# New places for out-projection and RWKV steps, two more MLP pairs ahead of their operands, and the second product's first split inside the last pair, in a hybrid layer

## Chip, cores and metric

The kernel runs on one core of a Trainium2 chip. The metric is the device time of one execution in microseconds; of several runs the median is shown. The engines are named as the profile names them: PE (matrix products), PEld (its weight loads), DVE (VectorE), ACT (ScalarE), POOL (GpSimd) and SP, whose queue issues nearly all transfers.

## What is computed

One layer on 1024 positions of width 1024, in float32. The input is normalised and projected to 3200 features in one product; four mixers of width 256 work on slices of them (chunked attention with a relative bias, HGRN2, RWKV-7, RG-LRU); their outputs are joined, projected back, normalised and added to the input; a squared-ReLU MLP with 4096 hidden features follows. Cut to the part around the change:

```python
mix = jnp.concatenate([ya, yb, yc, yd], axis=-1).astype(dt)
x = x + rms_norm(mix @ w_out[l], norm_mix_post[l])
h = rms_norm(x, norm_mlp_pre[l])
ff = jnp.square(jax.nn.relu(h @ mlp_w1[l])) @ mlp_w2[l]
x = x + rms_norm(ff, norm_mlp_post[l])
```

## The kernel before, in words

**Precision.** Every large product is made of three: each operand is split into a high part (a cast on ACT) and a low part (source minus high part, on DVE), and PE sums high x high, high x low and low x high into one PSUM bank (mm1, line 1159, for the MLP's first product; mm2 for its second). "Splitting" means that cast and that subtraction.

**Stages.** The 1024 positions are two halves of 512. For each half the mixers run (order RALH, then RHAL) and write their outputs to DRAM (mixd). part2 (line 1121) begins with the out projection: out_load (1049) fetches and splits the mixers' outputs of a half, out_mm (1060) multiplies, residual (1089) normalises and adds. For half 0, h2t (1281) transposes the result y0 into B1, eight pairs of split tiles. For half 1 the result is y1.

**The first MLP product** goes over 16 pairs of hidden tiles (a pair is two tiles of 128 features) by a scheme of seven products instead of eight over the 2 x 2 blocks of the operands (hidden tiles x inner index against the two halves of positions; Winograd's form). B1 is half 0's operand; Bt[0..4] are its sums and differences with half 1, made from y1 in the block marked T (lines 1336 to 1356): 32 transposes on PE, 36 sums and subtractions on DVE, 28 casts and scalings on ACT, the last of them for Bt[4]. Every product of 128 x 512 over half the inner index is 12 matmuls. A pair goes in steps: up_first (1200) loads the first weights, splits A11 and A12, and makes the product a, copied to s1; up_c11 (1210) adds the second product to a and gives h11; up_rest (1217) is a generator with five yields: split of s1's operand; product c with Bt[1], copied to s5 (line 1228); product b with Bt[2], s6 = s1 + b; product d with Bt[3], s5 += d; c with Bt[0], giving h21; d with Bt[4], then h22, h12 and the sums that the second product needs, each written to DRAM (put, 1179). w2_sums (1182) does sums of the second weights alongside. up_first and up_c11 need B1 alone, so for the first NFILL pairs they run ahead, while y1 is still on its way (fill, 1308); such a pair loads its first weights again later and its h11 back from DRAM.

**The second MLP product** (product, 1418) goes over seven block products of eight steps q. Each step loads two operands, splits both (split2, 1394) and makes 24 matmuls (lines 1414 to 1416).

**Memory.** Tiles come from pools; a tile tag with n buffers is a ring of n. Pool pw1 holds from part2 to the end: raw weights "wr" (4 buffers), split tiles "hl" (6), "s1" (6), "ho". Pool psc (1360) opens only after the raw inputs of T (raw0, raw1) are closed, and takes over their memory: s5, s6 (lines 1227, 1233), ho2, w2s, and more split tiles "hl2" (NHL3 = 2 before). hl (1138) counts the split tiles and sends them to one ring or the other:

```python
nhl[0] += 1
if hl2 and nhl[0] % (NHL + hl2[-1][1]) >= NHL:
    t = hl2[-1][0].tile([P, 2, 512], F32R, tag="hl2", name=nm(name), bufs=hl2[-1][1])
else:
    t = pw1.tile([P, 2, 512], F32R, tag="hl", name=nm(name), bufs=NHL)
```

**Order.** Every instruction has a place, its number in program order. A block entered with high_priority(offset=n) stands n places ahead; at(key) enters such a block with the offset that PRIO gives for the key (lines 56 to 61 and 102), and without an entry the offset is 0. A planner at build time goes through modelled time and gives each engine the ready instruction with the lowest place; what comes out is a fixed order for each engine, and each engine keeps its own. Keys that the change touches: "Om" + half (out_mm), "Rn" + half (rwkv's normalisation and gating, line 678), "U" + pair, and two new ones.

Of the kernel before, what the change touches and what calls it, by code (L numbers as in the profile page):

```python
# [43 lines left out]
GELU_C = math.sqrt(2.0 / math.pi)  # L44
DECAY_C = math.exp(-0.5)
PRIO_UP = 200
NFILL = 4
NWR, NHL, NHO, NS1, NHL2, NHL3, NHO2, NR2, NXR, NJ = 4, 6, 2, 6, 12, 2, 6, 8, 4, 2
KORD = ((0, 1, 2, 3, 4, 5, 6, 7), (4, 5, 6, 7, 2, 3, 0, 1))
PO0 = (("fm", "fm", "pa", "pa"), ("fm", "fm", "pa", "pa"))  # L50
PO1 = (("fm", "fm", "pa", "pa"), ("py", "fm", "pa", "ph"))
# [1 line left out]
NTAIL = 2  # L53
ORDER = ("RALH", "RHAL")

PRIO = {"A0": 30, "Ah01": 200, "Ah10": 100, "Ah11": 400, "Ah20": 60, "Ah30": 365, "At0": 700, "At1": 400, "Hf0": 40,
# [5 lines left out]
LEVELS = (32, 16, 8, 4, 2, 1)  # L62

VEC = {}
# [25 lines left out]
def body(ctx: ExitStack, tc: tile.TileContext, A: dict, out: bass.AP, dbg=None, stop_after=None):  # L90
# [11 lines left out]
    def at(*key):  # L102

        sec.close()
        n = PRIO.get("".join(map(str, key)), 0)
        if n:
            sec.enter_context(tc.high_priority(offset=n))

    def nm(base):
        uid[0] += 1  # L110
        return f"{base}_{uid[0]}"
# [1009 lines left out]
    def part2():  # L1121
# [10 lines left out]
        def raw(name):  # L1132
            return pw1.tile([P, 1024], F32, tag="wr", name=nm(name), bufs=NWR)
# [83 lines left out]
        def up_rest(p, r0, a, s1, w12):  # L1217
            if p < NFILL:
                r0 = w1load(2 * p)
            r1 = w1load(2 * p + 1)  # L1220
            A11, A12, A21, A22 = r0[:, 0:512], r0[:, 512:], r1[:, 0:512], r1[:, 512:]
            V.tensor_tensor(A21, A21, A22, ADD)
            w = parts(A21, "s1", V)
            yield
            c = bankm("pc_")
            mm1(c, w, Bt[1], True, True)
            s5 = psc.tile([P, 512], F32, tag="s5", name=nm("s5"), bufs=2)
            S.copy(s5[:], c[:])
            yield
            V.tensor_tensor(A21, A21, A11, SUB)  # L1230
            b = bankm("pb_")
            mm1(b, parts(A21, "s2", V), Bt[2], True, True)
            s6 = psc.tile([P, 512], F32, tag="s6", name=nm("s6"), bufs=2)
            V.tensor_tensor(s6[:], s1[:], b[:], ADD)
            yield
            V.tensor_tensor(A11, A22, A21, SUB)
            d = bankm("pd_")
            mm1(d, parts(A11, "s3", V), Bt[3], True, True)
            V.tensor_tensor(s5[:], s5[:], d[:], ADD)
            yield  # L1240
            if p >= NFILL:
                h11 = up_c11(p, a, w12)
            else:
                h11 = ho("ho")
                nc.sync.dma_start(h11[:], hx[0][p // 2][:, p % 2, :])
            V.tensor_tensor(A12, A12, A21, SUB)
            mm1(c, parts(A12, "s4", V), Bt[0], False, True)
            h21 = ho2("h21")
            V.tensor_tensor(h21[:], s6[:], c[:], ADD)
            relu2(h21[:], h21[:])  # L1250
            yield
            mm1(d, parts(A22, "w22", V), Bt[4], False, True)
            w2_sums(p)
            h22 = ho2("h22")
            V.tensor_tensor(h22[:], s6[:], s5[:], ADD)
            relu2(h22[:], h22[:])
            put(p, 3, h22)
            h12 = ho2("h12")
            V.tensor_tensor(h12[:], s6[:], d[:], ADD)
            relu2(h12[:], h12[:])  # L1260
            put(p, 1, h12)

            t1, t2, t4 = ho2("t1"), ho2("t2"), ho2("t4")
            V.tensor_tensor(t1[:], h21[:], h22[:], ADD)
            V.tensor_tensor(h21[:], h11[:], h21[:], SUB)
            V.tensor_tensor(t2[:], t1[:], h11[:], SUB)  # L1266
            V.tensor_tensor(t4[:], h12[:], t2[:], SUB)
            for i, t in ((4, t1), (6, h21), (5, t2), (2, t4)):
                put(p, i, t)
# [35 lines left out]

        fst = []

        def fill(n):

            for p in range(0, n, 2):  # L1310
                q = range(p, min(p + 2, n))
                for p in q:
                    fst.append(up_first(p))
                for p in q:
                    up_c11(p, fst[p][1], fst[p][3])

        with tc.high_priority(offset=PRIO_UP):
            fill(NFILL)
        part1.close()
        pb1_ = ctx2.enter_context(ExitStack())  # L1320
        pb1 = pb1_.enter_context(tc.tile_pool(name="pb1", bufs=1, reuse_waits="tile"))
# [6 lines left out]
        def bsplit(i, k, src, eng):  # L1328
            split(eng, Bt[i][k][0][:], Bt[i][k][1][:], src)

        gens = [up_rest(p, *fst[p]) for p in range(2)]
        with tc.high_priority(offset=PRIO_UP):
            for x in gens:
                next(x)
        kh = range(4)
        at("T")
        b12, b22 = [z[:] for z in raw1[0:4]], [z[:] for z in raw1[4:8]]
# [16 lines left out]
        for k in kh:  # L1354
            V.tensor_tensor(b11[k], b21[k], b11[k], SUB)
            bsplit(4, k, b11[k], V)
        at()
        raw1_.close()
        raw0_.close()
# [3 lines left out]
        while gens:  # L1363
            for x in list(gens):
                if next(x, 1):
                    gens.remove(x)
        for p in range(2, NHID // 2):
            at("U", p)
            for _ in up_rest(p, *(fst[p] if p < NFILL else up_first(p))):
                pass  # L1370
        at()
        ctx2.close()

# [15 lines left out]
        def load(src, name):  # L1389
            r = raw2(name)  # L1390
            nc.sync.dma_start(r[:], src)
            return r

        def split2(r, name):

            h, l = hl(name), hl(name)
            h_, l_ = (z[:].rearrange("p a b -> p (a b)") for z in (h, l))
            S.copy(h_, r[:])  # L1398
            V.tensor_tensor(l_, r[:], h_.bitcast(F32), SUB)  # L1399
            return h, l  # L1400

        W2 = lambda c: (lambda q: load(A["w2"][c, q], "wb"))
        TX = lambda i: (lambda q: load(tx[i][q][:].rearrange("p a b -> p (a b)"), "wt"))
# [14 lines left out]
        def product(i, right, banks, start, tail=0):  # L1418

            ops = {}  # L1420
            for q in range(NQ):
                x = split2(load(hx[i][q][:].rearrange("p a b -> p (a b)"), "ha"), "a2")
                ops[q] = x, split2(right(q), "b2")
                if q >= NQ - tail:
                    continue
                for t in range(4):
                    for n in range(2):
                        mm2(banks, *ops[q], t, n, start and q == 0 and n == 0, q == NQ - 1 and n == 1)
            for t in range(4):
                for q in range(NQ - tail, NQ):  # L1430
                    for n in range(2):
                        mm2(banks, *ops[q], t, n, False, q == NQ - 1 and n == 1)
                if tail:
                    yield t
# [195 lines left out]
```

## Time and profile before

| | us |
|---|---|
| median of 3 runs | 1336.4 |
| lowest and highest | 1330.17 and 1336.4 |
| the profiled execution, its own time | 1338.78 |
| its span, first to last instruction | 1337.0 |
| PE busy in the span | 1264.3 |
| mean granted clock of PE | 0.969 of full |

The profile is of one execution, and times within it are microseconds from the span's start. The mixers of both halves fill the first 620 us and more, the out projection runs from about 577 to 683, the first MLP product from 683 to 1014, the second from there to 1330. In the rows below, "<-" in brackets behind an instruction names what ended the idle time of its engine before it; matmuls overlap, so the duration of one is longer than the distance between two starts.

### The profile page before, as it was taken

The page shows a single profiled execution, that of the slowest core. Times are in us where ns is not written, and L with a number is a line of the kernel's source. Part 1 is how long each engine was busy: PE and PEld are TensorE (multiplying, and loading weights), DVE is VectorE, ACT ScalarE, POOL GpSimd, SP SyncE. Part 2 cuts the span into 40 slices and gives each one's busy share as a digit, 9 for nine tenths or more (in the row PEclk, how much of TensorE's full clock was granted, in tenths as well). Part 3 has the DMA queues.
Part 4 walks back from the last instruction along what each step waited for, and adds up shares of the span by engine and source line. Part 5 has one row for each costly group of instructions (what it writes and reads, how often), then busy time and mean ns, then how long its engine had stood idle before and what let it go on. Part 6 is the DMA issues. An engine that isn't in the chain of part 4 may idle for free. (4 is left out here: it accounts for less than half of the span.)

```text
span 1337.0 us, 21742 instructions
## 1 busy us (share of the span) xinstructions
PE 1264.3 (95%) x8424; PEld 995.1 (74%) x8424; DVE 852.7 (64%) x1538; ACT 662.0 (50%) x1171; POOL 83.7 (6%) x115
## 2 busy tenths in 40 slices
PE   6899999799999999998997999999998999999997
PEld 4677779566687777666786878888887888888886
DVE  4763647677553486765768878876775444444884
ACT  6633646466444344755766545454454433433441
POOL 1000010314102150000000000000000000000000
PEclk9898999889898999999998999999998999999999
DMA  7432112222122012334832888776656875666751
GB/s 261 137 95 74 34 63 93 81 67 92 41 86 70 18 56 74 91 120 139 312 136 76 287 296 267 265 267 233 214 197 241 322 257 194 194 192 197 262 227 63
DMA packets 101160, 213.66 MB, mean 160 GB/s; under 512 B 25281, under 2 KB 28993, under 8 KB 101057
## 3 DMA queue, kind: packets, MB, share of 16 engines
q1 hardware_dynamic: 101056, 212.27, 47.1%
q8 instruction: 66, 1.08, 0.3%
q14 instruction: 38, 0.30, 0.1%
HBM read 156.92 MB, written 55.31 MB: 159 GB/s over the span
## 5 line engine op out<-in xcount | busy, mean ns | idle before, releaser
L1414 PE MATMUL q<-b,a 128*128 128x512 f32 x448 | 175.8, 394 | 2.4 <-ACT b L1398 2.4
L1415 PE MATMUL q<-b,a 128*128 128x512 f32 x448 | 176.7, 394 | 1.3 <-DVE b L1399 1.3
L1416 PE MATMUL q<-b,a 128*128 128x512 f32 x448 | 176.4, 394 | 0.0
L324 PE MATMUL fm<-hh,wh 128*128 128x512 f32 x304 | 130.0, 430 | 13.2 <-ACT wh L182 8.0
L325 PE MATMUL fm<-hh,wl 128*128 128x512 f32 x304 | 128.0, 425 | 0.9 <-DVE wl L184 0.9
L326 PE MATMUL fm<-hl,wh 128*128 128x512 f32 x304 | 125.7, 419 | 0.5 <-DVE hl L253 0.5
L184 DVE TENSOR_TENSOR wl<-wr,wh 128x1024 fp32r<-128x1024 f32 x66 | 81.3, 1234 | 46.9 <-ACT wh L182 46.4
L182 ACT CAST wh<-wr 128x1024 fp32r<-128x1024 f32 x66 | 69.0, 1045 | 68.4 <-PE fm L326 37.6
L1414 PEld LDWEIGHTS q<-b,a 128*128 128x128 f32 x448 | 84.4, 189 | 21.4 <-ACT b L1398 2.8
L1415 PEld LDWEIGHTS q<-b,a 128*128 128x128 f32 x448 | 84.9, 189 | 20.5 <-DVE b L1399 1.7
L1416 PEld LDWEIGHTS q<-b,a 128*128 128x128 f32 x448 | 85.0, 190 | 18.9
L324 PEld LDWEIGHTS fm<-hh,wh 128*128 128x128 f32 x304 | 60.0, 198 | 31.2 <-ACT wh L182 8.5
L1399 DVE TENSOR_TENSOR b<-wb,b 128x1024 fp32r<-128x1024 f32 x32 | 39.2, 1224 | 60.8 <-ACT b L1398 60.6
L1398 ACT CAST b<-wb 128x1024 fp32r<-128x1024 f32 x32 | 33.5, 1048 | 79.8 <-PE q L1415 64.9
L325 PEld LDWEIGHTS fm<-hh,wl 128*128 128x128 f32 x304 | 60.2, 198 | 15.2 <-DVE wl L184 2.2
L1399 DVE TENSOR_TENSOR a<-ha,a 128x1024 fp32r<-128x1024 f32 x56 | 68.3, 1219 | 4.9 <-ACT a L1398 4.8
L326 PEld LDWEIGHTS fm<-hl,wh 128*128 128x128 f32 x304 | 59.6, 197 | 15.7 <-issue 3.0
L1149 ACT CAST s<-w 128x512 fp32r<-128x512 f32 x64 | 39.3, 619 | 60.5 <-DVE w L1230 19.6
L1399 DVE TENSOR_TENSOR b<-wt,b 128x1024 fp32r<-128x1024 f32 x24 | 29.4, 1225 | 55.9 <-ACT b L1398 55.9
L1398 ACT CAST a<-ha 128x1024 fp32r<-128x1024 f32 x56 | 58.6, 1046 | 7.1 <-DMA ha<-hx 7.1
L1398 ACT CAST b<-wt 128x1024 fp32r<-128x1024 f32 x24 | 25.2, 1048 | 73.5 <-PE q L1415 73.5
L365 PE MATMUL tm<-wh,hh 128*128 128x256 f32 x192 | 56.1, 292 | 3.5 <-DVE X L530 3.1
(1084 smaller groups left out, 2994.3 us busy)
## 6 DMA issues: line engine op xcount, KB each, us to landing
ha<-hx SPq DMA_DIRECT2D x56, 512.0 KB, 4.8
wr<-in_win_dram SPq DMA_DIRECT2D x50, 512.0 KB, 3.3
w<-in_w_dram SPq DMA_DIRECT2D x36, 512.0 KB, 4.9
wb<-in_w_dram SPq DMA_DIRECT2D x32, 512.0 KB, 6.8
wt<-tx SPq DMA_DIRECT2D x32, 512.0 KB, 3.6
w2s<-in_w_dram SPq DMA_DIRECT2D x48, 256.0 KB, 3.9
tx<-w2s SPq DMA_DIRECT2D x48, 256.0 KB, 2.2
hx<-h SPq DMA_DIRECT2D x48, 256.0 KB, 3.2
```

The lines of the kernel that those rows point to most:

```text
L182: S.copy(hi[:], raw[:])
L184: V.tensor_tensor(lo[:], raw[:], hi[:].bitcast(F32), SUB)
L324: T.matmul(ps[:], wh[:, ks], hi[:], start=(k == 0), stop=False, skip_group_check=True)
L325: T.matmul(ps[:], wl[:, ks], hi[:], start=False, stop=False, skip_group_check=True)
L326: T.matmul(ps[:], wh[:, ks], lo[:], start=False, stop=(k == NK - 1), skip_group_check=True)
L365: T.matmul(o, hi[:, tsl], wh[:, cs], start=(k == 0 and t % 2 == 0), stop=False, skip_group_check=True)
L1149: S.copy(t[:, 0, :], src)
L1398: S.copy(h_, r[:])
L1399: V.tensor_tensor(l_, r[:], h_.bitcast(F32), SUB)
L1414: T.matmul(o, ah[:, i, tsl], bh[:, i, :], start=start, stop=False, skip_group_check=True)
L1415: T.matmul(o, ah[:, i, tsl], bl[:, i, :], start=False, stop=False, skip_group_check=True)
L1416: T.matmul(o, al[:, i, tsl], bh[:, i, :], start=False, stop=stop, skip_group_check=True)
```

## The change

- PRIO has new entries: F 150, Om0 40, Om1 300, Rn1 368, U4 20, g 100; no old entry differs.
- NFILL goes from 4 to 6. The first four pairs are filled as before (NEARLY = 4, 200 places ahead); pairs 4 and 5 are filled in program order behind T, under the key "F". The first step of pairs 0 and 1 moves behind that, under the key "g", from ahead of T.
- s5 takes a tile of the ring "s1", which grows from 6 to 8 buffers, and s6 is the tile s1 itself. NHL3 grows from 2 to 3.
- In the last pair, after the fourth yield, ahead() loads the two operands of the second product's first step into "wr" tiles and splits them into four "hl" tiles, 60 places ahead. product takes them for its first step.

```diff
@@ -44,8 +44,9 @@
 GELU_C = math.sqrt(2.0 / math.pi)
 DECAY_C = math.exp(-0.5)
 PRIO_UP = 200
-NFILL = 4
-NWR, NHL, NHO, NS1, NHL2, NHL3, NHO2, NR2, NXR, NJ = 4, 6, 2, 6, 12, 2, 6, 8, 4, 2
+AHEAD = 60
+NFILL, NEARLY = 6, 4
+NWR, NHL, NHO, NS1, NHL2, NHL3, NHO2, NR2, NXR, NJ = 4, 6, 2, 8, 12, 3, 6, 8, 4, 2
 KORD = ((0, 1, 2, 3, 4, 5, 6, 7), (4, 5, 6, 7, 2, 3, 0, 1))
 PO0 = (("fm", "fm", "pa", "pa"), ("fm", "fm", "pa", "pa"))
 PO1 = (("fm", "fm", "pa", "pa"), ("py", "fm", "pa", "ph"))
@@ -53,12 +54,12 @@
 NTAIL = 2
 ORDER = ("RALH", "RHAL")
 
...
+        "F": 150,
...
+        "Om0": 40, "Om1": 300,
...
+        "Rn1": 368,
...
+        "U4": 20, "g": 100,
...
 LEVELS = (32, 16, 8, 4, 2, 1)
 
 VEC = {}
@@ -1224,13 +1225,13 @@
             yield
             c = bankm("pc_")
             mm1(c, w, Bt[1], True, True)
-            s5 = psc.tile([P, 512], F32, tag="s5", name=nm("s5"), bufs=2)
+            s5 = pw1.tile([P, 512], F32, tag="s1", name=nm("s5"), bufs=NS1)
             S.copy(s5[:], c[:])
             yield
             V.tensor_tensor(A21, A21, A11, SUB)
             b = bankm("pb_")
             mm1(b, parts(A21, "s2", V), Bt[2], True, True)
-            s6 = psc.tile([P, 512], F32, tag="s6", name=nm("s6"), bufs=2)
+            s6 = s1
             V.tensor_tensor(s6[:], s1[:], b[:], ADD)
             yield
             V.tensor_tensor(A11, A22, A21, SUB)
@@ -1305,9 +1306,9 @@
 
         fst = []
 
-        def fill(n):
-
-            for p in range(0, n, 2):
+        def fill(first, n):
+
+            for p in range(first, n, 2):
                 q = range(p, min(p + 2, n))
                 for p in q:
                     fst.append(up_first(p))
@@ -1315,7 +1316,7 @@
                     up_c11(p, fst[p][1], fst[p][3])
 
         with tc.high_priority(offset=PRIO_UP):
-            fill(NFILL)
+            fill(0, NEARLY)
         part1.close()
         pb1_ = ctx2.enter_context(ExitStack())
         pb1 = pb1_.enter_context(tc.tile_pool(name="pb1", bufs=1, reuse_waits="tile"))
@@ -1328,10 +1329,6 @@
         def bsplit(i, k, src, eng):
             split(eng, Bt[i][k][0][:], Bt[i][k][1][:], src)
 
-        gens = [up_rest(p, *fst[p]) for p in range(2)]
-        with tc.high_priority(offset=PRIO_UP):
-            for x in gens:
-                next(x)
         kh = range(4)
         at("T")
         b12, b22 = [z[:] for z in raw1[0:4]], [z[:] for z in raw1[4:8]]
@@ -1354,6 +1351,12 @@
         for k in kh:
             V.tensor_tensor(b11[k], b21[k], b11[k], SUB)
             bsplit(4, k, b11[k], V)
+        at("F")
+        fill(NEARLY, NFILL)
+        at("g")
+        gens = [up_rest(p, *fst[p]) for p in range(2)]
+        for x in gens:
+            next(x)
         at()
         raw1_.close()
         raw0_.close()
@@ -1364,10 +1367,27 @@
             for x in list(gens):
                 if next(x, 1):
                     gens.remove(x)
+        def parts2(r, h, l):
+
+            h_, l_ = (z[:].rearrange("p a b -> p (a b)") for z in (h, l))
+            S.copy(h_, r[:])
+            V.tensor_tensor(l_, r[:], h_.bitcast(F32), SUB)
+            return h, l
+
+        def ahead():
+
+            with tc.high_priority(offset=AHEAD):
+                for src in (hx[0][0][:].rearrange("p a b -> p (a b)"), A["w2"][0, 0]):
+                    r = raw("w2a")
+                    nc.sync.dma_start(r[:], src)
+                    first.append(parts2(r, *(pw1.tile([P, 2, 512], F32R, tag="hl", name=nm("a2"), bufs=NHL) for _ in range(2))))
+
+        first = []
         for p in range(2, NHID // 2):
             at("U", p)
-            for _ in up_rest(p, *(fst[p] if p < NFILL else up_first(p))):
-                pass
+            for n, _ in enumerate(up_rest(p, *(fst[p] if p < NFILL else up_first(p)))):
+                if p == NHID // 2 - 1 and n == 3:
+                    ahead()
         at()
         ctx2.close()
 
@@ -1393,11 +1413,7 @@
 
         def split2(r, name):
 
-            h, l = hl(name), hl(name)
-            h_, l_ = (z[:].rearrange("p a b -> p (a b)") for z in (h, l))
-            S.copy(h_, r[:])
-            V.tensor_tensor(l_, r[:], h_.bitcast(F32), SUB)
-            return h, l
+            return parts2(r, hl(name), hl(name))
 
         W2 = lambda c: (lambda q: load(A["w2"][c, q], "wb"))
         TX = lambda i: (lambda q: load(tx[i][q][:].rearrange("p a b -> p (a b)"), "wt"))
@@ -1419,8 +1435,12 @@
 
             ops = {}
             for q in range(NQ):
-                x = split2(load(hx[i][q][:].rearrange("p a b -> p (a b)"), "ha"), "a2")
-                ops[q] = x, split2(right(q), "b2")
+                if first:
+                    ops[q] = tuple(first)
+                    first.clear()
+                else:
+                    x = split2(load(hx[i][q][:].rearrange("p a b -> p (a b)"), "ha"), "a2")
+                    ops[q] = x, split2(right(q), "b2")
                 if q >= NQ - tail:
                     continue
                 for t in range(4):
```

## Rows read from the trace of the kernel before

**Rows 1.** Page, part 1: busy us, share of span, instructions by engine
```profile
PE 1264.3 (95%) x8424; PEld 995.1 (74%) x8424; DVE 852.7 (64%) x1538; ACT 662.0 (50%) x1171; POOL 83.7 (6%) x115
```

**Rows 2.** Windows: length, busy (count) of PE, PEld, DVE, ACT, POOL, clock, DMA, GB/s
```profile
1014.00:1027.00 13.00, 9.34 (x28) 6.84 (x27) 8.98 (x11) 6.85 (x9) 0.00 (x0) 0.74 0.83 293
1030.00:1043.00 13.00, 13.00 (x58) 10.69 (x57) 10.22 (x9) 7.75 (x8) 0.00 (x0) 1.00 1.03 411
683.50:705.50 22.00, 22.00 (x98) 18.16 (x98) 17.60 (x32) 17.70 (x41) 0.00 (x0) 1.00 0.46 156
705.50:742.00 36.50, 28.98 (x125) 22.43 (x123) 32.07 (x52) 21.39 (x39) 0.00 (x0) 0.86 0.37 122
744.00:774.00 30.00, 30.00 (x130) 24.23 (x130) 27.16 (x45) 15.43 (x28) 0.00 (x0) 1.00 0.88 303
774.00:800.00 26.00, 23.90 (x97) 18.90 (x96) 19.87 (x32) 11.90 (x21) 0.00 (x0) 0.93 0.84 283
```

**Rows 3.** PE's waits over the span: releaser, us in total, times, longest
```profile
PE pc__1090_7457 L1165 <- ACT s L1228: 5.9, 1, 5.9
PE po L1079 <- ACT mh L189: 5.0, 2, 3.8
...
PE pm L713 <- DVE ysb L703: 2.4, 1, 2.4
PE pa__1165_7946 L1165 <- ACT s L1207: 2.1, 1, 2.1
```

**Rows 4.** PE's timeline where the second product starts
```profile
1014.16 0.39 PE L1167 MATMUL pd__1438_9795<-bt4h,w 128*128 128x512 f32 x1
1016.93 1.20 PE L1414 MATMUL q<-b,a 128*128 128x512 f32 x4 [2.38 <-ACT b L1398]
1019.41 0.80 PE L1415 MATMUL q<-b,a 128*128 128x512 f32 x1 [1.28 <-DVE b L1399]
1020.00 0.63 PE L1416 MATMUL q<-b,a 128*128 128x512 f32 x1
1020.43 0.63 PE L1414 MATMUL q<-b,a 128*128 128x512 f32 x1
```

**Rows 5.** DVE's timeline in pair 15 and at the second product's start
```profile
1011.78 0.69 DVE L1249 TENSOR_TENSOR h<-s,pc__1433_9760 128x512 f32<-128x512 f32 x1 [4.78 <-PE pc__1433_9760 L1167]
...
1018.13 1.22 DVE L1399 TENSOR_TENSOR b<-wb,b 128x1024 fp32r<-128x1024 f32 x1
```

**Rows 6.** DVE's busy time while block T is made; clock, DMA, GB/s
```profile
706.00:731.00 25.00, 24.57 (x40) 0.95 0.14 38
```

**Rows 7.** Timeline of all engines where T begins
```profile
700.30 0.72 ACT L1119 ACTIVATE yo<-yo,mrs 128x512 f32<-128x512 f32 x1
...
705.58 0.38 PE L1284 MATMUL h<-ident,yo 128*128 128x128 f32 x2
```

**Rows 8.** Timeline of all engines where T ends
```profile
715.98 0.39 PE L1165 MATMUL pb__1092_7473<-bt2h,s 128*128 128x512 f32 x1
...
728.86 0.62 ACT L189 CAST bt4h<-raw 128x512 fp32r<-128x512 f32 x1 [1.79 <-DVE raw L1355]
729.38 0.58 ACT L1228 COPY s<-pc__1088_7442 128x512 f32<-128x512 f32 x1
...
732.34 0.68 DVE L1150 TENSOR_TENSOR s<-w,s 128x512 fp32r<-128x512 f32 x1
```

**Rows 9.** DVE's timeline ahead of pair 4
```profile
778.81 0.69 DVE L1189 TENSOR_TENSOR w2s<-w2s 128x512 f32<-128x512 f32 x1 [3.21 <-DMA w<-in_w_dram]
```

**Rows 10.** ACT's timeline, second half of the mixers
```profile
488.05 1.28 ACT L787 ACT_TABLE_LOAD   x1
489.34 0.63 ACT L787 ACTIVATE z<-z 128x512 f32<-128x512 f32 x1
```

**Rows 11.** DMA issues: operation, count, KB each, median us to landing
```profile
wr<-in_win_dram SPq DMA_DIRECT2D x50, 512.0 KB, 3.3
w<-in_w_dram SPq DMA_DIRECT2D x36, 512.0 KB, 4.9
```

More of the change, by code (lines that the diff above doesn't have):

```diff
@@ L54 @@
 ORDER = ("RALH", "RHAL")
-PRIO = {"A0": 30, "Ah01": 200, "Ah10": 100, "Ah11": 400, "Ah20": 60, "Ah30": 365, "At0": 700, "At1": 400, "Hf0": 40,
[5 rows of a table removed]
+PRIO = {"A0": 30, "Ah01": 200, "Ah10": 100, "Ah11": 400, "Ah20": 60, "Ah30": 365, "At0": 700, "At1": 400, "F": 150,
[5 rows of a table added]
 LEVELS = (32, 16, 8, 4, 2, 1)
```

10 rows, old and new, of the table PRIO are left out of this document.

## Prediction

> **What bounds the kernel now.** I read the page's busy times first: PE is busy for 1264.3 of 1337.0 us, VectorE (DVE) and ScalarE (ACT) for 64% and 50% [rows 1]. So time can be won only where PE stands still or runs at its lower clock, and the windows say where. From 1030 on PE starts 58 matmuls in 13 us at full clock [rows 2]; I price a matmul of 512 columns at 13 / 57 = 0.228 us. With that price three stretches behind the mixers are short of work [rows 2]: 705.5 to 742 (125 matmuls, of which 32 are short transposes at about 0.1 us: 93 x 0.228 + 3 = 24.2 us of work in 36.5, **12.3 us lost**), 774 to 800 (97 x 0.228 = 22.1 of 26, **3.9 lost**), 1014 to 1027 (28 x 0.228 = 6.4 of 13, **6.6 lost**). The list of PE's waits names releasers: 5.9 us for an ACT copy of line 1228, 2.1 us for one of line 1207, and ahead of these stretches 3.8 us for the casts of the mixers' outputs and 2.4 us for RWKV's last product [rows 3]. A loss is larger than its wait because the clock falls behind it: after PE stood for 2.38 and 1.28 us at the start of the second product, matmuls start 0.43 us apart [rows 4], which is the lower level of 1.2 GHz.
>
> **Part 1, the second product's first step.** Pair 15's last matmul starts at 1014.16 [rows 4]. The next needs four splits (a cast on ACT and a subtraction of 1.22 us on DVE for each operand), and the last of the subtractions starts at 1018.13, between the pair's last sums [rows 5]. The change puts two loads of 512 KB and these splits behind step 4 of pair 15, 60 places early. They fit there: DVE waits 4.78 us for one product [rows 5]. The price is four of six "hl" tiles; the pair's last two splits then wait until the products before them have released theirs, which in program order still leaves each a product of 12 x 0.228 = 2.7 us ahead of its use. The two loads stand on SP's queue in front of the pair's last stores and cost two issues. What is late next is step q=1: its splits take the places that q=0 had, so the last ends near 1018.13 + 1.22 = 1019.4, while PE, starting q=0 at 1014.4, needs it at 1014.4 + 24 x 0.228 = 1019.9. Gain at most 6.6; at least 3.0, if the wait moves to q=1 or q=2 and is halved. I take **-6.0**, near the upper end because q=1 just makes it.
>
> **Part 2, pairs 4 and 5 early.** 48 matmuls, 48 x 0.228 = 10.9 us, leave the later loop and go into the stretch where the transformed activations (block T) are made. T is DVE's: it is busy for 24.57 of the 25 us from 706 to 731 [rows 6]. The extra work helps only if PE does it while DVE makes T; if PE does it before T's transposes, T starts later by as much and nothing is won. Places in program order decide: T has 96 instructions, its first at -10 (PRIO 10); the new fill (66 instructions) stands behind T and goes 150 ahead, from 96 - 150 = -54 to +12. Its two first products (36 instructions) and 8 matmuls of the next come before T, the rest among T's first transposes. y1 is ready at 701.0 (the scaling at 700.30 takes 0.72), so T is free to start; it now begins at 705.58 behind four pairs of fill [rows 7], and would begin 24 x 0.228 + 8 x 0.228 = 7.3 us later. Of 10.9 us moved, 3.6 are won. Bounds: nothing (all before T) and 10.9 (all beside T). I take **-3.6**, from the count of places. The splits of pairs 4 and 5 add four subtractions of about 0.6 us to DVE ahead of T, where it is busy for 17.60 of 22 us [rows 2]. On SP's queue two weight loads and two stores now stand ahead of the four loads of pairs 0 and 1, whose first step goes from 200 places ahead to "g", place 96 + 66 - 100 = 62 beside T's own. That step's splits (s1) have the same gaps of DVE before T as cover; without it, c would wait for them up to the two thirds of T that stand ahead of place 62, and the 3.6 would be lost.
>
> **Part 3, s5 and s6 out of the late pool.** The 5.9 us wait is for the copies of c at 729.38; c was complete before 715.98, where the next product starts [rows 8]. The copy's tile lay in the pool that takes over the memory of T's raw inputs, so it ran behind T's last cast at 728.86. In the change s5 takes an "s1" tile, s6 is s1 itself, and this wait goes. But the ring counter of split tiles changes too. Once the late pool is open it takes each split whose number, modulo 8, is 6 or 7. The first four pairs' fill counts to 8 and s1 to 10, so the numbers are 14 and 15, s3 of the second pair and s4 of the first, and two splits do run late, from 732.34 on [rows 8]. In the change the fill counts to 12, s1 to 14, and the modulus is 9: 15, 16 and 17 go there, s2 of both pairs and s3 of the first. So a new wait stands in the old one's place: ACT's cast and DVE's subtraction of s2 wait for T, and behind them PE's products b, b and d. Before T ends PE has five products in either case (now c, c, b, b, d; then c, c, d and both with bt0). I take **0**, with two products, 5.5 us, either way.
>
> **Part 4, reloads.** A filled pair loads its first weights and its h11 again: 2 x 512 + 2 x 256 KB, 1.6 MB, at 303 GB/s [rows 2] 5.2 us of transfers. They lie beside PE work unless they are late; PE's 2.1 us wait is such a case: DVE stood 3.21 us for a load [rows 9], the sums of w2 came late, and behind them what PE needed. That wait may stay with pair 4, move to pair 6 or repeat: **0**, between -3.9 and +7.8 (two more such losses).
>
> **Part 5, places.** Om0, Om1, U4 and Rn1 move instructions that stay the same. Om1 cannot bring the mixers' last outputs sooner, so the 3.8 us stay unless other work fills them. Rn1's chain hangs on RWKV's last product, so only what stands ahead of it on DVE can go: part of 2.4 us [rows 3]. Against that, a square root brought between exponentials costs tables: a load takes 1.28 us, and the next ACT instruction starts 0.01 us behind it [rows 10]; one more pair is 2.6 us. I take **-1.0**, between -6.2 (3.8 and 2.4) and +2.6. The Trainium skill ("ScalarE: Activation LUTs", section "What ACT_TABLE_LOAD costs") states about 2.66 us for each switch, a drain included; by an estimate from that, one more pair is 5.3 us, and a sum with it in this term's place is -4.3 where the trace's 2.6 gives -7.0. The trace shows no drain behind the load.
>
> **Sum:** -6.0 - 3.6 + 0 + 0 - 1.0 = -10.6. The profiled execution took 1338.8 us (span 1337.0 and 1.8 around it), so 1328.2 on its scale; the median of the three runs shown, 1336.4, is 2.4 lower, so **1326 us**.
>
> **Rivals.** (A) The early work is only moved: T starts 10.9 us later and the new wait eats the rest; only the second product gains: 1336.4 - 6 = 1330. For it: y1 is ready before the old fill ends. Against it: T's first transposes have places ahead of most of the second half of the new fill. That the change does not do what its name says belongs here: no place of HGRN's own steps differs in the diff. (B) All loss of the T stretch goes: -12.3 - 6.0 - 1.0 gives 1317. For it: line 1228's wait is named and removed. Against it: s2 in the late pool. (C) Slower: pairs 2 to 5 have 72 x 0.228 = 16.4 us of PE work each where others have 21.9, with the same transfers, and DVE is busy for 27.16 of 30 us there already [rows 2]; if the wait of [rows 9] comes at four pairs and not at one, that is 3 x 3.9 = +11.7, with nothing won in T and 3.0 at the second product: 1345. Two more waits would leave it near no change; it decides from the third on. For it: loads of 512 KB land in 3.3 us in the mixers and 4.9 in this loop [rows 11], so load makes them late. The Trainium skill ("DMA: Bandwidth & Descriptors", section "Latency and other measured facts") gives 0.2 us on average and 2 us at high load for HBM's access latency; the trace's 1.6 us more agrees. Against it: between 744 and 774, at 303 GB/s, PE has no gap [rows 2], and pairs without first products run there.
>
> **How the numbers follow.** Forecast 0.50, A 0.25, B 0.13, C 0.12. Half a percent, about what a measurement of this kernel can tell from no change, is 6.7 us: faster is below 1329.7. Faster: 0.47 of the forecast, and B, 0.60; same: A and 0.03 of the forecast, 0.28; slower: C, 0.12. The range reaches from B with the loss at 774 gone too (1336.4 - 12.3 - 6.6 - 3.9 = 1314) to 1339, where T wins nothing, the second product 3.0 and one or two more pairs wait; it leaves out C and little else.
>
> **What would show it.** Right: no wait of PE over 1 us between pair 15 and the second product, and full clock there; the copies of line 1228 a few us behind their products; T's transposes 5 to 10 us later than the fourth pair's fill ends. Wrong: casts of s2 behind bt4's last cast with PE standing before b; PE waiting at q=1 or q=2; waits for line 1207 or 1222 at several pairs between 745 and 830.

## The result, and the profile after

The changed kernel takes 1321.4 us (median of 6 runs, 1313.2 to 1325.0), the kernel before 1335.2 beside it: ratio 0.990, 95% interval 0.986 to 0.994, **faster by 1.0%**. The forecast was 1326.0 (1314 to 1339). The two profiled executions differ by the same 13.8 us (1338.8 and 1325.0). Four stretches between landmarks on PE's timeline show where they come from: the first product of the fill, pair 6's first product with bt1 (all pairs whose first products are moved are done by then), the second product's first matmul, and its last. PE's timeline of the kernel before (start, duration, engine, line, operation, tiles; its row of 1016.93 stands in [rows 4]; the row of 748.98, and of 755.36 after, is pair 2's first product with bt1 and is used further down):

```profile
683.77 0.40 PE L1165 MATMUL pa__1053_7112<-b1h,w 128*128 128x512 f32 x1
...
748.98 0.39 PE L1165 MATMUL pc__1125_7690<-bt1h,s 128*128 128x512 f32 x1
...
822.48 0.40 PE L1165 MATMUL pc__1217_8293<-bt1h,s 128*128 128x512 f32 x1
...
1329.17 0.39 PE L1416 MATMUL q<-b,a 128*128 128x512 f32 x1
```
And of the kernel after:

```profile
682.43 0.40 PE L1166 MATMUL pa__1053_7112<-b1h,w 128*128 128x512 f32 x1
...
755.36 0.39 PE L1166 MATMUL pc__1135_7766<-bt1h,s 128*128 128x512 f32 x1
...
815.41 0.39 PE L1166 MATMUL pc__1215_8295<-bt1h,s 128*128 128x512 f32 x1
...
1007.39 0.39 PE L1430 MATMUL q<-a,a 128*128 128x512 f32 x1
...
1315.31 0.40 PE L1432 MATMUL q<-b,a 128*128 128x512 f32 x1
```

| stretch, us | before | after | difference |
|---|---|---|---|
| start to the fill | 683.8 | 682.4 | -1.3 |
| fill to pair 6 | 138.7 | 133.0 | -5.7 |
| pair 6 to the second product | 194.4 | 192.0 | -2.5 |
| second product | 312.2 | 307.9 | -4.3 |

The last two are part 1: 6.8 us (499.9 us together; x2_fill below, which has no part 1, took 506.0, so against it 6.1). The second is parts 2 to 4, the first part 5 (with a reservation in the last section).

The windows of after that answer to [rows 2] (the same columns):

```profile
705.50:742.00 36.50, 30.64 (x133) 24.32 (x132) 33.82 (x55) 25.62 (x47) 0.00 (x0) 0.91 0.34 111
774.00:800.00 26.00, 25.34 (x110) 20.26 (x109) 24.37 (x40) 13.13 (x23) 0.00 (x0) 1.00 0.95 327
1014.00:1027.00 13.00, 13.00 (x58) 10.70 (x57) 7.35 (x7) 6.30 (x6) 0.00 (x0) 1.00 1.01 377
```

From 1014 to 1027 PE now starts 58 matmuls at full clock where it started 28 at 0.74. From 774 to 800 it starts 110 and not 97, with the clock at 1.00. From 705.5 to 742 the gain is small (133 and 125), and DVE is busy for 33.82 of 36.5 us. The list of PE's waits answers to [rows 3] (releaser, us in total, times, longest):

```profile
PE po L1080 <- ACT mh L190: 5.3, 1, 5.3
...
PE pc__1100_7520 L1168 <- DVE s L1151: 4.0, 1, 4.0
```

The 5.9 us at line 1228 and the 2.1 us at line 1207 are gone, and so are the 2.4 us for RWKV's last product; the wait for the mixers' casts grew from 3.8 to 5.3, and a new wait of 4.0 us stands in pair 0's product with bt0. How T begins and ends in after, in the order of time (answers to [rows 7, 8]):

```profile
704.24 3.65 PE L1285 MATMUL h<-ident,yo 128*128 128x128 f32 x32
...
709.26 0.50 PE L1166 MATMUL pa__1085_7429<-b1h,w 128*128 128x512 f32 x1 [1.36 <-ACT raw L1340]
...
720.28 0.40 PE L1166 MATMUL pc__1100_7520<-bt1h,s 128*128 128x512 f32 x1
...
730.06 0.62 ACT L190 CAST bt4h<-raw 128x512 fp32r<-128x512 f32 x1 [0.58 <-DVE raw L1352]
...
730.56 0.68 DVE L1151 TENSOR_TENSOR s<-w,s 128x512 fp32r<-128x512 f32 x1
...
730.59 1.66 ACT L1150 CAST s<-w 128x512 fp32r<-128x512 f32 x3
...
731.29 0.79 PE L1168 MATMUL pc__1100_7520<-bt0h,s 128*128 128x512 f32 x1 [4.04 <-DVE s L1151]
...
732.31 0.63 PE L1166 MATMUL pb__1104_7551<-bt2h,s 128*128 128x512 f32 x1
```

T's 32 transposes come first, at 704.24, and the 48 matmuls of pairs 4 and 5 behind them, from 709.26 to 720.28. Two products c follow, then two matmuls of pair 0's product with bt0; there PE stands until 731.29. Its releaser, the subtraction at 730.56, stood on DVE among the last ones of bt4. In PE's order the products b come next, and the casts of their splits (730.59, three in one row) run right behind bt4's last cast at 730.06: the late tiles of the prediction's part 3. Matmuls then start 0.43 us apart until 735.8, the lower level of 1.2 GHz.

### The profile page after: what moved, and what is told of

It is laid out like the page before. It is cut to its first block, busy times and chain, and to the rows that moved or that the text cites. A ratio compares the mean times of both kernels' runs of the same rounds, so it can differ in the third digit from the quotient of the medians.

```text
span 1323.2 us, 21759 instructions
## 1 busy us (share of the span) xinstructions
PE 1257.9 (95%) x8424; PEld 992.5 (75%) x8424; DVE 847.7 (64%) x1538; ACT 661.7 (50%) x1171; POOL 82.3 (6%) x115
## 5 line engine op out<-in xcount | busy, mean ns | idle before, releaser
L1430 PE MATMUL q<-b,a 128*128 128x512 f32 x440 | 172.4, 392 | 0.0
L1431 PE MATMUL q<-b,a 128*128 128x512 f32 x440 | 172.2, 391 | 0.0
L1432 PE MATMUL q<-b,a 128*128 128x512 f32 x440 | 172.2, 391 | 0.0
L1432 PEld LDWEIGHTS q<-b,a 128*128 128x128 f32 x440 | 82.6, 188 | 18.4
L1431 PEld LDWEIGHTS q<-b,a 128*128 128x128 f32 x440 | 82.6, 188 | 18.3
L1430 PEld LDWEIGHTS q<-b,a 128*128 128x128 f32 x440 | 82.6, 188 | 18.2
```

The lines of the kernel that those rows point to most:

```text
L1430: T.matmul(o, ah[:, i, tsl], bh[:, i, :], start=start, stop=False, skip_group_check=True)
L1431: T.matmul(o, ah[:, i, tsl], bl[:, i, :], start=False, stop=False, skip_group_check=True)
L1432: T.matmul(o, al[:, i, tsl], bh[:, i, :], start=False, stop=stop, skip_group_check=True)
```

## The experiments

Each ratio is to runs of the kernel before on the same chip, where it took 1334.1 to 1336.7 us; the times of runs on different chips are compared only as roughly as that. "Fill to pair 6" is the stretch of the table above, in the one profiled execution of each run. How much it scatters is seen from before and x1_first_step, which are the same kernel there: 138.7 and 138.9.

| run | time, us | ratio to before, 95% interval | fill to pair 6 |
|---|---|---|---|
| before | 1335.2 | | 138.7 |
| the change | 1321.4 | 0.990 (0.986 to 0.994) | 133.0 |
| x1_first_step | 1330.1 | 0.996 (0.9935 to 0.9986) | 138.9 |
| x2_fill | 1330.6 | 0.9965 (0.9935 to 0.9996) | 130.4 |
| x3_places | 1333.4 | 0.9988 (0.9963 to 1.0014) | 139.0 |
| x4_ring | 1319.7 | 0.9889 (0.9856 to 0.9922) | 132.9 |
| y1_no_u4 | 1320.1 | 0.9846 (0.98 to 0.9892) | 131.3 |
| y2_ring_no_u4 | 1318.7 | 0.9878 (0.9846 to 0.991) | 134.2 |
| y3_ahead_of_t | 1326.7, one run | | 135.8 |
| y4_s5s6 | 1334.2, one run | | 141.6 |
| z1_late_sums | **1307.3** | **0.9788 (0.975 to 0.9826)** | 124.1 |
| z2_late_sums_only | 1316.7 | 0.9871 (0.983 to 0.9913) | 131.1 |
| z3_four | 1325.3 | 0.9925 (0.9895 to 0.9954) | 139.4 |
| z4_four_late | 1317.3 | 0.9859 (0.9815 to 0.9903) | 130.5 |

The stretch's own floor, by the prediction's price: 43 products of 12 matmuls at 0.228 us and T's transposes, 3.65 us, are 121.3 us.

**Each part alone.** The first three runs divide the change.

x1_first_step is the kernel before with this (and ahead() and parts2() of the diff):

```diff
         for p in range(2, NHID // 2):
-            for _ in up_rest(p, *(fst[p] if p < NFILL else up_first(p))):
-                pass
+            for n, _ in enumerate(up_rest(p, *(fst[p] if p < NFILL else up_first(p)))):
+                if p == NHID // 2 - 1 and n == 3:
+                    ahead()
```

> The kernel before with part 1 alone (loads and splits of the second product's first step behind step 4 of pair 15). Theory: the parts are independent, and this one gives what the trace of the change shows between pair 15's last product and the second product, 6.9 us: 1335.2 - 6.9 = 1328. No wait of TensorE between the two, clock 1.00 from 1014 to 1027. Rival: part of the 6.9 us hangs on the other parts (pair 15 there starts 7 us earlier, its stores are out of the way); alone the step comes late by one split and the gain is 3 to 4: 1332.

It gained 5.3 us (1.9 to 8.7 by the interval), between the two, and the trace shows the theory's amount: no wait of PE at the step, and from pair 6 to the second product's last matmul 499.8 us where before took 506.7. The row of the window answers to [rows 2]:

```profile
1000.00:1030.00 30.00, 30.00 (x132) 24.54 (x131) 15.07 (x18) 12.88 (x18) 0.00 (x0) 1.00 0.71 257
```

x2_fill is the change without part 1 and without four places:

```diff
-                if p == NHID // 2 - 1 and n == 3:
-                    ahead()
...
-"Om0": 40, "Om1": 300, "Rn1": 368, "U4": 20
```

> The kernel before with pairs 4 and 5 filled early, s5 and s6 out of the late pool, 8 s1 tiles and 3 late split tiles, with the two places F and g, but without part 1 and without the places Om0, Om1, Rn1, U4. Theory: 3.1 us in the stretch of block T and 2.6 us at pairs 4 to 6, 1335.2 - 5.7 = 1329.5; TensorE still stands some 4 us for a subtraction of line 1151 near 729. Rival: the 2.6 us come from U4, which puts pair 4 ahead by 20 places, and not from the early products: the 2.1 us wait at pair 4 is still there or has moved, and the time is 1332.

4.7 us, with an interval from 0.5 to 8.7. The fill to pair 6 shrank by 8.3 us, more than in the whole change. PE's waits show the theory's 4.0 us and nothing for pair 4, so U4 was not what removed that wait; the 2.4 us at the second product, which part 1 takes away, are still there:

```profile
PE pc__1100_7520 L1163 <- DVE s L1146: 4.0, 1, 4.0
...
PE q L1424 <- ACT b L1368: 2.4, 1, 2.4
```

x3_places is the kernel before with the places:

```diff
+"Om0": 40, "Om1": 300, "Rn1": 368, "U4": 20
```

> The kernel before with the four places Om0, Om1, Rn1 and U4 alone. Theory: 1.4 us, 1335.2 - 1.4 = 1333.8, not to be told from no change: the wait for RWKV's last product (2.4 us) and the wait of the transposes of line 1284 (1.5 us) go, the wait for the mixers' outputs grows from 3.8 to some 5.3 us. Rival: U4 alone also removes the 2.1 us wait at pair 4 and the slow clock behind it, 3.9 us more: 1330.

1.6 us less, not to be told from no change: the theory. Its waits are the theory's too, and with U4 alone the wait at pair 4 stays:

```profile
PE po L1074 <- ACT mh L184: 5.2, 2, 4.9
...
PE pa__1165_7946 L1160 <- ACT s L1202: 2.4, 1, 2.4
```

**The new wait.** x4_ring is the change with the counter of split tiles moved:

```diff
+nhl[0] += 3
 hl2.append((psc, NHL3))
```

> The changed kernel with the counter of split tiles set 3 further when the late pool opens, so that s2 of pairs 0 and 1 and s3 of pair 0 get tiles that are free at once, and the last splits of these pairs get the late ones. Theory: the 4.0 us wait at 727 and the lower clock until 735 come from those three splits, which wait for the memory of block T's inputs; b follows c without a gap, and 5 to 7 us go: 1321.4 - 6 = 1315. Rival: VectorE, busy without a break from 706 to 735, is the bound of this stretch; TensorE then waits for the low halves of bt3 or bt0 instead, and the time stays at 1321 (plus or minus 2).

Both hold in part. The wait at 727 is gone, and the window from 706 to 745 has 166 matmuls at full clock where the change has 142 at 0.91. From T's last transpose to pair 1's last product it takes 40.3 us instead of 47.9. But by pair 6 nothing is left (132.9 and 133.0). The window of x4_ring:

```profile
706.00:745.00 39.00, 38.33 (x166) 31.17 (x167) 37.03 (x62) 27.99 (x53) 0.00 (x0) 1.00 0.38 123
```

And its PE waits in pairs 2 to 4:

```profile
PE pc__1173_8020 L1166 <- ACT s L1150: 3.0, 1, 3.0
...
PE pd__1158_7927 L1168 <- DVE s L1151: 1.6, 1, 1.6
...
PE pd__1139_7800 L1166 <- DVE s L1240: 1.4, 1, 1.4
```

y1_no_u4 is the change without one place; y2_ring_no_u4 is the same with the edit of x4_ring besides:

```diff
-"U4": 20
```

> The changed kernel without the place U4 (pair 4 no longer 20 places ahead). From the first product of the fill to pair 6's first product c the change takes 133.0 us, and the run with parts 2 to 4 alone, which has no U4, took 130.4. Theory: U4 mixes pairs 4 and 5 and costs those 2.6 us: 130.4 again, in all 1321.4 - 2.6 = 1319. Rival: the difference is an accident of when the loads come; 133.0 and 1321.

131.3, nearer the theory: U4 costs 1.7 us in this stretch of the trace; the times (1320.1 and 1321.4) can't show so little.

> The changed kernel with the ring counter 3 further and without U4. With the counter alone block T's stretch was 7.5 us shorter (from T's last transpose to pair 0's last product 37.6 us instead of 45.1), and all of it was given back by pair 6 (132.9 us from the fill to pair 6, before 133.0), at waits of 1.4, 1.6 and 3.0 us in pairs 2 to 4. Theory: they come from U4, as in the run beside this, so 126 to 128 us from the fill to pair 6 and 1321.4 - 6 = 1315. Rival: pairs 2 to 5 are bound by VectorE and their loads (VectorE busy 97 to 102 us of these 107 to 116 in every version), and what T gains is given back there whatever the places: 130 to 133, and 1319 to 1321.

The rival: 134.2 and 1318.7. What T gained is given back without U4 as well, and now at two waits of PE, of 2.0 and 3.2 us. Both stand behind the w2 sums, which are three loads, three subtractions (lines 1185 to 1187) and three stores for each pair. SP's waits from 755 to 767:

```profile
SPq L1189 <- DVE w2s L1185: 1.3, 1, 1.3
...
SPq L1184 <- DMA tx<-w2s: 0.8, 2, 0.6
```

The timeline of DVE, SP and PE there, in the order of time:

```profile
758.58 0.69 DVE L1185 TENSOR_TENSOR w2s<-w2s 128x512 f32<-128x512 f32 x1 [0.36 <-issue]
...
759.79 0.68 DVE L1186 TENSOR_TENSOR w2s<-w2s 128x512 f32<-128x512 f32 x1
...
760.99 0.69 DVE L1187 TENSOR_TENSOR w2s<-w2s 128x512 f32<-128x512 f32 x1
761.59 0.69 DVE L1146 TENSOR_TENSOR s<-w,s 128x512 fp32r<-128x512 f32 x1
...
762.33 0.50 PE L1163 MATMUL pd__1158_7927<-bt3h,s 128*128 128x512 f32 x1 [2.00 <-DVE s L1146]
...
763.88 1.28 SPq L1184 DMA_DIRECT2D w2s<-in_w_dram  x3
...
765.21 0.43 SPq L1193 DMA_DIRECT2D w<-in_w_dram  x1
...
773.80 0.69 DVE L1218 TENSOR_TENSOR w<-w 128x512 f32<-128x512 f32 x1
...
775.19 0.50 PE L1161 MATMUL pc__1173_8020<-bt1h,s 128*128 128x512 f32 x1 [3.24 <-ACT s L1145]
```

The first wait is DVE's: the subtraction of 761.59, which ends pair 3's split and PE's 2.00 us, stands behind all three w2 subtractions of another pair. The second is of two parts. The load of the weights ("w") that pair 4's c needs goes out at 765.21, behind loads of w2 sums that wait for the stores of the sums before them, and lands 6.1 us later, at 771.3. DVE has four other instructions in front from 771.20 on, two of them w2 subtractions, and begins the sum of these weights at 773.80; PE stands for 3.24 us until 775.19. How far a wait holds SP's queue is seen right behind these loads: from 766.8 on SP issues nothing for 5.1 us, until the subtraction of a w2 sum that it is to store is done.

```profile
SPq L1189 <- DVE w2s L1186: 5.6, 3, 5.1
```

(This row is of SP's waits from 740 to 780.) The Trainium skill ("DMA: Bandwidth & Descriptors", section "Anatomy of one DMA — SWDGE (gpsimd) path") says that a semaphore is waited for on the issuing sequencer and not by the DMA engines; the 5.1 us agree.

y3_ahead_of_t is the change with all six pairs filled in front:

```diff
-NFILL, NEARLY = 6, 4
+NFILL, NEARLY = 6, 6
```

> The changed kernel with all six pairs filled where four were, ahead of block T in the program, so that their product banks are handed out ahead of those of T's transposes. Theory: it was the ring of eight banks, not the places, that put T's transposes in front of the products of pairs 4 and 5 (their first bank is the one of T's first transposed tile); with the banks handed out first, the 48 products run ahead of T, T starts 10.9 us later, and from the fill to pair 6 it takes 138 to 141 us instead of 133.0. Rival: it makes no difference whether PE does them ahead of T or beside it, 133 again.

Its PE timeline at the first product of the fill and at T's first transposes:

```profile
681.73 0.40 PE L1166 MATMUL pa__1053_7112<-b1h,w 128*128 128x512 f32 x1
...
714.42 3.65 PE L1285 MATMUL h<-ident,yo 128*128 128x128 f32 x32
```

T's transposes start 714.42 - 681.73 = 32.7 us behind the fill's start; in the change 704.24 - 682.43 = 21.8. So they come 10.9 us later, the price of all 48 matmuls (which the expectation calls products), as the theory has it. The edit also gives all of the two pairs' instructions places ahead of T, so this run alone does not tell banks from places; the wait at 709.26 in the change does (see the section on why). The price is smaller than it expected, 2.8 us and not 5 to 8. PE's longest wait in the stretch is then one of 5.5 us, for bt0; what else makes up for the delay was not followed.

y4_s5s6 is the kernel before with 8 s1 tiles and

```diff
-            s5 = psc.tile([P, 512], F32, tag="s5", name=nm("s5"), bufs=2)
+            s5 = pw1.tile([P, 512], F32, tag="s1", name=nm("s5"), bufs=NS1)
...
-            s6 = psc.tile([P, 512], F32, tag="s6", name=nm("s6"), bufs=2)
+            s6 = s1
```

> The kernel before with s5 in an s1 tile and s6 in place of s1 (8 s1 tiles) alone; ring of split tiles as before. Theory: the 5.9 us wait for the copy of line 1228 goes, but the two late split tiles are still s3 of pair 1 and s4 of pair 0, so only one product more can run before T ends: 2 to 3 us from the fill to pair 6 (138.7 before), 136. Rival (that the late copies were the whole of it): 5.9 us and the slow clock behind it, 130 to 131.

Neither: 141.6, 2.9 us longer than before. T itself gained what the rival said, 5.0 us (from its last transpose to pair 1's last product 35.1 us, before 40.1), and by pair 6 it had given back 7.9, at waits for the splits of pair 2 (2.3, 2.2 and 1.4 us), the longest of which is

```profile
PE pd__1127_7722 L1167 <- DVE s L1150: 2.3, 1, 2.3
```

**What gives it back, and what the early pairs are worth.** Four runs cross these two. z1_late_sums is y2_ring_no_u4 with the edit below, z2_late_sums_only is y1_no_u4 with it:

```diff
-            w2_sums(p)
+            if p >= NFILL:
+                w2_sums(p)
 ...
             mm1(d, parts(A11, "s3", V), Bt[3], True, True)
+            if NFILL <= p < 2 * NFILL:
+                w2_sums(p - NFILL)
```

> The run before with the ring counter 3 further and no U4, and besides the sums of w2 for the six filled pairs (three loads, three subtractions, three stores each) made in pairs 6 to 11, two sets a pair. Theory: what T gained was given back because pairs 2 to 4 wait for their own weights, whose loads stand on SP's queue behind loads and stores of the w2 sums (the c of pair 4 stood 3.2 us); without the sums no wait over 1 us between 740 and 800, 126 to 128 us from the fill to pair 6 instead of 134.2, pairs 6 to 15 at most 1 us longer, 1318.7 - 7 = 1312. Rival 1: the loads wait for free weight tiles and not for the queue; 132 to 134 and 1318. Rival 2: pairs 6 to 11 lose what pairs 2 to 4 win (from pair 6 to the second product 198 us instead of 192), 1318.

More than the theory: 124.1 us, 2.8 above the floor, and **1307.3 us**, the fastest kernel of this study. PE has no gap between 700 and 800, and pairs 6 to 15 took 191.8 us, no longer than in the change. Not all sums went where the edit puts them, for the planner brings some forward again: of the 18 w2 subtractions that y2_ring_no_u4 makes between the fill and pair 6, z1_late_sums still makes 6 there. The rows of one of their three lines, first of y2_ring_no_u4 and then of z1_late_sums:

```profile
L1185 DVE TENSOR_TENSOR w2s<-w2s x6: 684/691/693, 730.5 to 801.5; 128x512 f32<-128x512 f32 x6
```

```profile
L1185 DVE TENSOR_TENSOR w2s<-w2s x2: 682/688/695, 745.5 to 776.4; 128x512 f32<-128x512 f32 x2
```

Its windows, and after them the two landmarks on its PE timeline:

```profile
700.00:740.00 40.00, 40.00 (x175) 32.49 (x174) 36.05 (x60) 27.00 (x51) 0.00 (x0) 1.00 0.40 143
740.00:800.00 60.00, 60.00 (x260) 48.70 (x259) 57.97 (x96) 33.56 (x59) 0.00 (x0) 1.00 0.84 286
```

The landmarks:

```profile
668.47 0.40 PE L1161 MATMUL pa__1053_7112<-b1h,w 128*128 128x512 f32 x1
...
792.59 0.40 PE L1161 MATMUL pc__1209_8235<-bt1h,s 128*128 128x512 f32 x1
```

> The changed kernel without U4 (1320.1) with the late w2 sums, ring counter as in the change. Theory: here T's 4.0 us wait sets when pairs 0 and 1 end, and TensorE has no wait over 0.3 us in pairs 2 to 5, so the late sums win nothing or up to 2 us: 130 to 131 from the fill to pair 6 (131.3 without them), 1319. Rival: VectorE, with 11 us less to do before pair 6, ends T sooner, and 4 us or more go: 127 and 1316.

131.1, the theory: without the ring the late sums win 0.2 us. So with six pairs filled the two edits work only together: ring alone +2.9 us (131.3 to 134.2), late sums alone -0.2, both -7.2. Part of that is that the edit did less here: 12 of the 18 subtractions are still made ahead of pair 6.

z3_four is y1_no_u4 with four pairs filled, and z4_four_late is z3_four with the late sums:

```diff
-NFILL, NEARLY = 6, 4
+NFILL, NEARLY = 4, 4
```

> The changed kernel without U4 and with four filled pairs instead of six; s5, s6, the ring of 9 and the places stay, so that the late split tiles fall to s4 of both pairs and a later one, and c, b and d of both pairs can run before T ends. Theory: the two early pairs are not what matters; with the ring out of the way T has as much work of TensorE beside it as with them (six products, 16.4 us), and some of it is given back in pairs 2 to 4 for late weights: 132 to 135 from the fill to pair 6, against 131.3 with six pairs and 138.7 before; 1323. Rival: the 48 products moved beside T are what won; without them 138 to 139 and 1328.

139.4, the rival: without the 48 matmuls all of the gain before pair 6 is gone. Waits of 4.3 us in pair 1 and of 2.5 and 2.8 us in pair 2 take its place.

> The run before with four filled pairs, and with the w2 sums of these four made in pairs 4 to 7. Theory: of the 139.4 us that four pairs took from the fill to pair 6, some 8 are waits of pairs 2 and 3 (2.5 and 2.8 us and the slow clock behind them) for weights that stand behind the w2 sums on SP's queue; they go, the stretch of T stays as it was (36.2 us from T's last transpose to pair 1's end), and 131 to 132 us and 1317 are left: then the early pairs are worth the 7 us to the 124.1 of six pairs with late sums and with the ring. Rival: pairs 2 and 3 wait for free weight tiles, whatever else the queue holds, and it is 138 to 139 and 1325 again.

130.5, the theory to within half a microsecond; in the list of its PE waits only T's is left over 1 us in the stretch:

```profile
PE pd__1098_7527 L1161 <- DVE s L1237: 4.3, 1, 4.3
```

With the sums in place pairs 4 and 5 filled early are therefore worth 8.1 us (139.4 to 131.3). With late sums and the counter as in the change nothing is seen of that: 130.5 with four pairs, 131.1 with six (z2_late_sums_only), each with 12 w2 subtractions in the stretch. Only six pairs with the counter moved as well (z1_late_sums) are 6.4 us better than four with late sums, and four pairs with the counter moved were not run. In all of these the number of filled pairs also shifts which splits are late, since eight are counted instead of twelve, so that none of the three figures is of the early products alone. What the late sums free was not divided further: in z1_late_sums they take loads and stores from the queue, bytes from the DMA engines and some 8 us of subtractions (12 of 0.68 us) from DVE, and DVE is still busy for 57.97 of 60 us there.

## Why the prediction was right, and where it was not

The total was near (-10.6 forecast, -13.8 measured), and faster was right. Its terms held less well.

**Part 1 was right.** -6.0 taken, 6.8 in the change's trace (6.1 against x2_fill), 6.9 in x1_first_step's, about the upper end of 6.6. The step that decided it, that q=1 just makes it, held with the 0.5 us to spare that it had worked out: the last subtraction of q=1 ends at 1012.36, and q=1 starts right behind q=0 at 1012.85. DVE's and PE's timeline of the kernel after:

```profile
1011.14 1.22 DVE L1374 TENSOR_TENSOR b<-wb,b 128x1024 fp32r<-128x1024 f32 x1
...
1012.85 0.40 PE L1430 MATMUL q<-b,a 128*128 128x512 f32 x1
```

**Part 2 failed at the step by which T "would begin 24 x 0.228 + 8 x 0.228 = 7.3 us later", from the count of places.** They were not delayed at all. Whatever the places said, the banks had the say: the first product of pair 4 needs a bank, eight are handed out in turn, four pairs and the eight transposed tiles take the first twelve, and the thirteenth is that of T's first transposed tile. PE's wait of 1.36 us at 709.26 names it: the ACT copy of line 1340 that reads this tile, and that gives the matmul none of its operands. Its weights were ready: the last of the twelve splits of the six pairs ends on DVE at 700.35, before T's first transpose.

```profile
699.66 0.69 DVE L1151 TENSOR_TENSOR w<-w,w 128x512 fp32r<-128x512 f32 x1 [0.68 <-ACT w L1150]
```

y3_ahead_of_t hands the banks out in the other order (and moves the places with them) and gets the 10.9 us of delay. The Trainium skill ("PSUM — Partial Sum Buffer", section "Specifications (TRN2)") gives 8 banks per partition, so no larger ring was to be had; no run here tried one. All 10.9 us of them thus ran beside T, 7.3 more than forecast. In the change's own setting, sums in place and counter unmoved, the pairs were worth 8.1 us (z3_four against y1_no_u4), between the -3.6 taken and the bound of -10.9.

**Part 3 named the wait and mis-sized it.** That s2 of both pairs and s3 of the first would run behind bt4's last cast is what the three casts at 730.59 show. The step that failed is "before T ends PE has five products in either case": it had two and two matmuls of a third, since the subtraction of s4 was placed among T's last ones, and d behind b in PE's order. Three products fewer are, by the price of 2.7 us each, an estimated 8.2 us, more than the two products (5.5 us) that the prediction allowed, against the 7.3 that part 2 had too little. **The sum of the two (-3.6 taken, -3.2 measured up to pair 2's first product) was right because the errors cancelled, which is luck.**

**Part 4 is the term that was most off in the total.** 0 was taken. Up to pair 2's first product the change is 3.2 us ahead (before 65.2 us from the fill and 10.9 for the 48 matmuls, after 72.9), which is parts 2 and 3; the other 2.5 of the 5.7 us are pairs 2 to 5, where the 2.1 us wait and the slow clock behind it went, on the side of the lower bound. But in y2_ring_no_u4 two waits came in these pairs, of 2.0 and 3.2 us. That is near rival C's mechanism (the w2 sums come late, and behind them what PE needs): here the first wait comes of the order of DVE's instructions, the second of that order and a late load of weights. Such waits decide as soon as T no longer holds these pairs up: each of x4_ring, y2_ring_no_u4 and y4_s5s6 removed a wait in T and lost the gain in pairs 2 to 5.

**Part 5 is not contradicted in size, but its time is not shown** (-1.0 taken; x3_places gave 1.6 with an interval that takes in no change; from the end of the wait for the mixers' casts to the fill the change takes 50.6 us, before 52.2). Its reason held in part: the 3.8 us did not go but grew, the 2.4 us went. The rest came from a wait that it had not listed, 1.5 us for line 1284. No table load was added (23 in either trace, each 1.28 us), so that the Trainium skill's dearer switch ("ScalarE: Activation LUTs", section "What ACT_TABLE_LOAD costs") was not put to the test.

Rival A fell with z3_four against y1_no_u4: the early work was not only moved. Rival B asked for what z1_late_sums comes near to, 124.1 us where the floor is 121.3, but the change does not reach it.

## What to carry to other kernels

Before a place in the order is counted, write down the ring that hands out the tile or bank: who had the tile before decides, whatever the priority. Where a wait is removed ahead of a stretch that another engine or a queue nearly fills, list there what is not needed soon and yet stands ahead of what is: here the w2 sums, on DVE and on the in-order queue of SP. The gain stood only when most of them were moved to where there was room, and the runs do not tell which of the two counted more. When an edit shifts a ring's phase, as a changed number of filled pairs does here, a difference between two runs is of both. A sum that comes out right is not a proof of its terms; a run with one part alone is.

## What the runs showed that was not expected

The mixers' time varies from run to run with no change in them. In z1_late_sums every engine has the same order of instructions as in the change up to block T, yet the fill starts at 668.5 and not at 682.4, 14 us sooner: from 250 to 450 PE was granted more of its clock. The windows of the change (columns as in [rows 2]):

```profile
250.00:345.00 95.00, 85.56 (x619) 60.45 (x619) 70.33 (x150) 51.55 (x112) 27.16 (x31) 0.91 0.20 66
345.00:450.00 105.00, 95.76 (x1317) 78.69 (x1320) 50.45 (x122) 45.99 (x83) 14.04 (x21) 0.89 0.22 62
```

The windows of z1_late_sums:

```profile
250.00:345.00 95.00, 86.27 (x690) 60.27 (x688) 72.89 (x152) 53.98 (x117) 29.62 (x31) 0.98 0.21 70
345.00:450.00 105.00, 98.27 (x1463) 80.51 (x1462) 53.94 (x139) 48.30 (x91) 15.09 (x22) 0.93 0.20 59
```

What made the difference in the grant was not tried. The 1.3 us of the first table's first row are therefore no measure of part 5. It also means that two profiled executions compare stretch by stretch, and that of the 24 us between these two only 8.9, the stretch from the fill to pair 6, belong to the edits; the medians differ by 14.1.
